# Scores of two heads at once on the halves of TensorE's rows, in float32r parts, with the masks ahead of them

## The chip, the cores and the metric

The kernel runs on one core of a Trainium2 chip, in one launch. The metric is the device time of that core in microseconds (us). Five engines work side by side, each on its own queue of instructions: TensorE (PE in the rows; PEld is its weight load, PEq or PEldq its sequencer), VectorE (DVE), ScalarE (ACT), GpSimd (POOL) and SyncE (SP).

## The reference, cut to what matters

A network of four blocks works on x, 512 tokens of 1024 numbers in float32. The first two blocks (a convolution with a linear recurrence, and differential attention, each followed by a gated feed-forward layer) come first; then two layers follow, each a mixing layer and a layer of experts (MoE) with a layer norm behind each. A mixing layer has sixteen heads of 64 numbers, four of each of four kinds; the three kinds that the change touches are these (the fourth, latent attention or MLA, stays in float32):

```python
def _stick_breaking_attention(q, k, v):            # 4 heads
    z = jnp.einsum('bhqd,bhkd->bhqk', qb, k).astype(jnp.float32) * scale
    before = kpos[None, :] < qpos[:, None]
    log_keep = jnp.where(before, jax.nn.log_sigmoid(-z), 0.0)
    ...
def _forgetting_attention(q, k, v, log_f):         # "Fox", 4 heads
    s = jnp.einsum('bhqd,bhkd->bhqk', qb, k).astype(jnp.float32) * scale
    return s + cb[..., :, None] - c[..., None, :]  # then a causal softmax
    ...
def _dilated_attention(qs, ks, vs):                # 4 heads, 3 branches
    for (window, dil), q, k, v in zip(((128, 1), (512, 4), (2048, 16)), qs, ks, vs):
        idx = qpos[:, None] - dil * jnp.arange(window // dil + 1)[None, :]
        z = jnp.einsum('bqhd,bqnhd->bhqn', qb, kb).astype(jnp.float32) * scale
        p = jnp.exp(jnp.where(valid[None, None], z, -jnp.inf) - m)
    ...
x = _layernorm(DN_ALPHA * x + _mixing(x, ...), ...)
x = _layernorm(DN_ALPHA * x + _hier_moe(x, ...), ...)
```

Queries and keys of the dilated heads are rotated by position (rope) first. Depthwise convolution in the first block has 31 taps.

## The kernel before

Names: P = 128 rows, T = 512 tokens, D = 1024, NT = 4 tiles of tokens, `xs` the four tiles of x (128x1024 each).

**Products in parts.** `split` (L212, L213) writes a float32 tile as two float32r parts: ScalarE copies the high part, VectorE subtracts it to get the low part. `mm3` (L261 to L263) multiplies in three passes, high by high and the two cross terms. Projections, feed-forward and experts run so. The differential attention (L844) has its q and k in parts as well: the two maps of a head lie on rows 0 to 63 and 64 to 127, each pass is issued for the one and then the other, into two PSUM banks, and the masks (L846) follow. `diff_head` is not changed.

**A mixing layer.** `section` projects three times 256 columns: q of four heads, k of four heads, and v. Head h has its q and k on rows 64 (h % 2) and up of column h // 2. `rope2` rotates a projected column with VectorE and GpSimd and writes it into one float32 tile `qk` of `quads`. Scores are then single float32 products over 64 rows: `scores` (L1219, dilated branches 1 and 2, four 128-column tiles in a bank, each with a mask product L1220 behind it), `scores2` (L1238 to L1243, branch 0, two query tiles in a bank), `softmax_heads.scores` (L1524, then the forget row L1526 and the mask L1527; MLA uses it too without the row) and `stick_breaking.scores` (L1563). A mask is a bfloat16 product with the identity. After the scores `exp_rows` takes the maximum on VectorE (L1150) and the exponential on ScalarE (L1155); then TensorE transposes (L1162) and multiplies by v.

**Order.** In the mixing layers TensorE's order is written by hand (`manual_schedule`). `weave` and `fill` lay the small steps of the attention between the projections of the next section, by the costs that `pipelined` is given. The other engines are ordered by the scheduler. PSUM has eight banks; `self.ps("s")` takes the next of a cycle, and before the change "s" and "t" have two banks each. `late_ln` applies the gain of the layer norm before (`gain`, L467, L468) to the four tiles of x on VectorE while the first section runs. At the layer's end `out_add` (L1369) adds the output projection to x.

**Other places.** `conv` block (L608 to L630) does 11 taps of each of four blocks of channels on TensorE, by diagonal matrices that GpSimd (L624) and ScalarE (L625) make, and the rest as VectorE operations (L629). `moe_last` ends a MoE layer: 16 products with a 0/1 matrix `place` (L1838) put the last experts' rows back in order, VectorE adds them to x in halves (L1842), and the layer norm's statistics (L350) follow. Ahead of it stands a branch on how many blocks of tokens there are (L1823). `x<-acc` are DMAs of 512 KB on GpSimd's queue that bring a tile of x from DRAM.

## Time and profile before

| | us |
|---|---|
| median of 3 runs | 2835.93 (2834.44 to 2836.62) |
| the profiled execution | 2840.61 |
| its span | 2838.5 |
| TensorE busy | 2711.8 (96%) |
| VectorE busy | 1661.8 (59%) |
| ScalarE busy | 1292.0 (46%) |
| GpSimd busy | 456.8 (16%) |

In the span, the convolution lies at 20 to 175 us, the two mixing layers at about 1215 to 1650 and 2025 to 2460, and the two MoE layers behind them. A row of the timeline is a run of like instructions of one engine: start, length, line, result and operands, shape, count, and in brackets how long the engine had been idle and what released it. Matmuls overlap and their ends are modelled; the cost of one is the distance from its start to the next start.

### The profile page before, as it was taken

How to read it: one execution, taken by the hardware profiler on the slowest of the kernel's cores; microseconds unless marked ns; L12 is line 12 of the kernel's file. 1: busy time of each engine (PE TensorE's matmuls, PEld its weight loads, DVE VectorE, ACT ScalarE, POOL GpSimd, SP SyncE). 2: the span in 40 equal slices, each digit the busy share in tenths (PEclk: the TensorE clock that was granted, in tenths of full speed). 3: DMA queues.
4: the chain of work that ended last, by engine and by line, in shares of the span. 5: the costliest groups of instructions: out<-in, count | busy, mean ns of one | idle time of the engine just before them, and what ended most of it. 6: DMA issues, size and time to landing. Idle time of an engine off the chain costs nothing. (4 is left out here: it accounts for less than half of the span.)

```text
span 2838.5 us, 40948 instructions
## 1 busy us (share of the span) xinstructions
PE 2711.8 (96%) x14416; PEld 2250.9 (79%) x14416; DVE 1661.8 (59%) x2598; ACT 1292.0 (46%) x2020; POOL 456.8 (16%) x410
## 2 busy tenths in 40 slices
PE   8989999999999999999999969999899999799995
PEld 6768888887678888898877768888787787688885
DVE  7785333377864333464345587578743344756897
ACT  4643222255643222243364336568534544346785
POOL 2314000011113000011020042112101120412113
PEclk9999999999999999999999979999899999899998
DMA  6114323222114223222211058979412111278995
GB/s 222 47 45 163 104 82 104 89 102 79 60 53 141 100 86 104 89 75 75 70 40 60 18 206 278 287 237 332 149 60 86 45 69 33 104 242 258 356 359 197
DMA packets 90248, 376.56 MB, mean 133 GB/s; under 512 B 14352, under 2 KB 15760, under 8 KB 73488
## 3 DMA queue, kind: packets, MB, share of 16 engines
q1 hardware_dynamic: 76304, 329.14, 32.9%
q0 software_dynamic: 11104, 38.93, 5.4%
q10 hardware_dynamic: 2592, 5.49, 0.6%
q8 instruction: 117, 1.92, 0.3%
q14 instruction: 131, 1.07, 0.1%
HBM read 344.96 MB, written 28.57 MB: 132 GB/s over the span
## 5 line engine op out<-in xcount | busy, mean ns | idle before, releaser
L213 DVE TENSOR_TENSOR wpart<-raw,wpart 128x1024 fp32r<-128x1024 f32 (+3 forms) x385 | 519.0, 1378 | 315.9 <-ACT wpart L212 306.8
L212 ACT ACTIVATE wpart<-raw 128x1024 fp32r<-128x1024 f32 (+3 forms) x393 | 446.2, 1170 | 393.8 <-PE mm L262 175.6
L261 PE MATMUL mm<-xT,wpart 128*128 128x512 f32 (+1 forms) x1136 | 443.5, 390 | 12.2 <-ACT wpart L212 8.2
L263 PE MATMUL mm<-xT,wpart 128*128 128x512 f32 (+1 forms) x1136 | 429.3, 378 | 3.1 <-DVE wpart L213 3.1
L262 PE MATMUL mm<-xT,wpart 128*128 128x512 f32 (+1 forms) x1136 | 429.7, 378 | 1.3 <-DVE xT L213 1.3
L261 PEld LDWEIGHTS mm<-xT,wpart 128*128 128x128 f32 x1136 | 216.3, 190 | 51.5 <-ACT wpart L212 8.2
L261 PE MATMUL mm<-wpart,xT 128*128 128x256 f32 (+2 forms) x672 | 256.0, 381 | 0.0
L263 PEld LDWEIGHTS mm<-xT,wpart 128*128 128x128 f32 x1136 | 215.8, 190 | 47.6 <-DVE wpart L213 3.9
L262 PEld LDWEIGHTS mm<-xT,wpart 128*128 128x128 f32 x1136 | 216.5, 191 | 40.9 <-DVE xT L213 2.3
L263 PE MATMUL mm<-wpart,xT 128*128 128x256 f32 (+2 forms) x672 | 241.8, 361 | 0.2 <-DVE xT L213 0.2
L262 PE MATMUL mm<-wpart,xT 128*128 128x256 f32 (+2 forms) x672 | 240.6, 358 | 0.0
L343 POOL TENSOR_TENSOR sm<-sm,mhalf 128x4 f32<-128x4 f32 (+2 forms) x74 | 65.9, 892 | 1069.1 <-DVE sm L354 768.5
L262 PE MATMUL mm<-wpart,gT 128*128 128x256 f32 (+1 forms) x544 | 183.8, 338 | 0.0
L263 PE MATMUL mm<-wpart,gT 128*128 128x256 f32 (+1 forms) x544 | 183.2, 337 | 0.0
L261 PE MATMUL mm<-wpart,gT 128*128 128x256 f32 (+1 forms) x544 | 183.1, 337 | 0.0
L261 PEld LDWEIGHTS mm<-wpart,xT 128*128 128x128 f32 x672 | 145.2, 216 | 19.9 <-issue 7.7
L263 PEld LDWEIGHTS mm<-wpart,xT 128*128 128x128 f32 x672 | 145.0, 216 | 13.8 <-DVE xT L213 1.4
L262 PEld LDWEIGHTS mm<-wpart,xT 128*128 128x128 f32 x672 | 145.5, 217 | 10.1 <-issue 1.2
L544 DVE TENSOR_TENSOR silu<-silu,mm 128x512 f32<-128x512 f32 x44 | 30.2, 687 | 203.0 <-PE mm L263 203.0
L213 DVE TENSOR_TENSOR xT<-raw,xT 128x1024 fp32r<-128x1024 f32 x108 | 130.1, 1221 | 15.2 <-ACT xT L212 14.6
L1150 DVE TENSOR_REDUCE sm<-s 128x1 f32<-128x128 f32 (+3 forms) x96 | 53.3, 555 | 119.7 <-PE s L1220 45.7
L212 ACT ACTIVATE xT<-raw 128x1024 fp32r<-128x1024 f32 x108 | 111.8, 1053 | 8.2 <-DMA raw<-in_w_dram 7.6
(549 smaller groups left out, 5739.4 us busy)
## 6 DMA issues: line engine op xcount, KB each, us to landing
raw<-in_w_dram SPq DMA_DIRECT2D x324, 512.0 KB
raw<-in_gu_dram SPq DMA_DIRECT2D x40, 1024.0 KB
raw<-in_w_in_dram SPq DMA_DIRECT2D x30, 1024.0 KB
raw<-in_down_dram SPq DMA_DIRECT2D x16, 1024.0 KB
raw<-in_o_qk_dram SPq DMA_DIRECT2D x8, 1024.0 KB
raw<-in_w_out_dram SPq DMA_DIRECT2D x8, 1024.0 KB
raw<-in_e_in_dram SPq DMA_DIRECT2D x7, 1024.0 KB
raw<-in_down_dram SPq DMA_DIRECT2D x8, 768.0 KB
```

Of the source, the lines that this page charges most:

```text
L212: ins = self.nc.scalar.activation(hi, x, AF.Copy)
L213: self.last_lo = (eng or self.nc.vector).tensor_sub(lo, x, hi)
L261: mm(out, lhsT=ls[0], rhs=rs[0], start=start, stop=False)
L262: mm(out, lhsT=ls[0], rhs=rs[1], start=False, stop=False)
L263: mm(out, lhsT=ls[1], rhs=rs[0], start=False, stop=stop)
L343: self.last_rsqrt = self.nc.gpsimd.tensor_tensor(v, v, self.half[:, :n], op=ALU.pow)
L544: nc.vector.tensor_mul(s, s, ps[2 * j + 1])
L1150: nc.vector.tensor_reduce(nm, s.rearrange("p (n c) -> p n c", n=n), axis=AX, op=ALU.max, negate=True)
```

## The change

1. `section` keeps q and k as float32r parts in four tiles per buffer and two buffers; `rope2` and the plain sections end in a `split`.
2. `scores3` does the scores of two heads at once: masks first (with `start=True`), then three passes for each place, head by head in turn on rows 0 to 63 and 64 to 127, into two banks. Dilated branches and Fox use it; the odd head's part is kept in `waiting` until its turn. The stick-breaking heads take three passes one head at a time.
3. After the first section "s" and "t" share one cycle of four banks.
4. x goes to DRAM after `gain` (`lend_x`) and its tiles serve as buffers; `return_x` brings it back from GpSimd's queue, tiles 0 and 1 in `mla_heads.forget`, 2 and 3 after the last turned tile.
5. The last block of the convolution does 15 taps on TensorE instead of 11.
6. `moe_last` adds half 0 of x into PSUM by four float32 products with the identity ahead of the place products; statistics and normalisation read that half from PSUM, and VectorE adds half 1 only.
7. Masks are laid out anew and loaded in eight pieces instead of five; the layer norm's rows come as two tiles.

```diff
-NBUF = 15
+NBUF = 11
...
-    add("m_causal", np.where(k <= q, 0, neg))
...
-    add("m_all", np.full((P, P), neg))
+    causal = np.where(k <= q, 0, neg)
+    add("m_first", np.concatenate([np.full((P, P), neg), causal], axis=1))
+    _CF["m_causal"] = (_CF["m_first"][0] + P, P)
+    add("m_band", np.concatenate([np.where(k >= q, 0, neg), causal], axis=1))
...
-            raw = pool.tile([P, nm // 5], F32, name="rawc")
-            for h in range(5):
-                cs = slice(h * nm // 5, (h + 1) * nm // 5)
+            raw = pool.tile([P, nm // 8], F32, name="rawc")
+            for h in range(8):
+                cs = slice(h * nm // 8, (h + 1) * nm // 8)
...
-        for h, x in enumerate(self.x_halves(i)):
+        for h, x in enumerate(self.x_sources(i)):
...
+    def x_sources(self, i):
+        return [self.sums.get((i, h), x) for h, x in enumerate(self.x_halves(i))]
...
+    def norm_halves(self, i, rs, nm):
+        for src, x in zip(self.x_sources(i), self.x_halves(i)):
+            self.nc.scalar.activation(x, src, AF.Identity, bias=nm, scale=rs)
+        self.sums.pop((i, 0))
...
+        taps = PTAPS + (4 if j == 3 else 0)
+        n = T + taps - 1
...
-        for k in range(PTAPS):
+        ws = [pool.tile([P, PTAPS + 4], F32R, tag=f"taps{i}", name=self.uid("taps"))[:, :taps] for i in range(2)]
+        self.split(*ws, self.cols[:, _COLS["conv_w"] + j * 31:_COLS["conv_w"] + j * 31 + taps])
+        for k in range(taps):
...
-            self.mm3(ps, d, [t[:, k:k + T] for t in pads], k == 0, k == PTAPS - 1)
-        nc.vector.tensor_scalar(cv, pad[:, PTAPS:PTAPS + T], w(PTAPS), self.col("conv_b", j), op0=ALU.mult, op1=ALU.add)
-        for k in range(PTAPS + 1, 31):
+            self.mm3(ps, d, [t[:, k:k + T] for t in pads], k == 0, k == taps - 1)
+        nc.vector.tensor_scalar(cv, pad[:, taps:taps + T], w(taps), self.col("conv_b", j), op0=ALU.mult, op1=ALU.add)
+        for k in range(taps + 1, 31):
...
-            self.free, self.quads, self.outs = tiles(NBUF, [T]), tiles(3, [4, T]), tiles(4, [1056])
+            self.free, self.outs = tiles(NBUF, [T]), tiles(4, [1056])
...
                 self.weave(s1.steps)
+                self.bank["s"] = self.bank["t"] = cycle(range(2, 6))
                 gain()
-                s2 = self.section(xT, (3, 4, 5), rope=True, classes=True)
+                self.lend_x()
+                s2 = self.section(xT, (3, 4, 5), 1, rope=True, classes=True)
...
+    def quad_tile(self, n, j, shape, dtype=F32):
+        return self.pool.tile([P] + shape, dtype, tag=f"quad{n}{j}", name=self.uid("qd"))
...
+    def lend_x(self):
+        self.x_kept = self.dram.tile([T, D], F32, name=self.uid("xk"))
+        for i, x in enumerate(self.xs):
+            self.nc.gpsimd.dma_start(self.x_kept[i * P:(i + 1) * P, :], x)
+        self.lent = [x for i in range(2) for x in self.x_halves(i)]
+        self.spare = [x for i in range(2, NT) for x in self.x_halves(i)]
+        self.free += self.spare
+    def return_x(self, tiles):
+        for i in tiles:
+            self.nc.gpsimd.dma_start(self.xs[i], self.x_kept[i * P:(i + 1) * P, :])
...
+            parts = r.qk[j][:, 0], r.qk[j][:, 1]
             if rope:
-                self.rope2(ps[j], r.qk[:, j], classes, 0.125 if j < 2 else 1.0)
+                self.rope2(ps[j], parts, classes, 0.125 if j < 2 else 1.0)
             elif j < 2:
-                nc.scalar.activation(r.qk[:, j], ps[j], AF.Copy, scale=0.125)
+                self.split_scaled(*parts, ps[j], 0.125)
             else:
-                nc.vector.tensor_copy(r.qk[:, j], ps[j])
+                self.split(*parts, ps[j])
...
-        u = (t, sh)
-        if parts:
-            nc.vector.tensor_add(t, *u)
-            self.split(*out, t)
-            self.drop(sh, t)
-            return
+        nc.vector.tensor_add(t, t, sh)
         if classes:
-            out = out.rearrange("p (r j) -> p j r", r=4)
-            u = [x.rearrange("p (j r) -> p j r", r=4) for x in u]
-        nc.vector.tensor_add(out, *u)
+            parts = [x.rearrange("p (r j) -> p j r", r=4) for x in parts]
+            self.split(*parts, t.rearrange("p (j r) -> p j r", r=4))
+        else:
+            self.split(*parts, t)
         self.drop(sh, t)
+    def scores3(self, banks, h, qk, place, mask):
+        mm = self.nc.tensor.matmul
+        q, k = qk[h // 2], qk[2 + h // 2]
+        for m, s in enumerate(banks):
+            mask(h + m, s)
+        for cs, qs, ks in place:
+            for n, (a, b) in enumerate(((0, 0), (0, 1), (1, 0))):
+                for m, s in enumerate(banks):
+                    rows = slice(64 * m, 64 * m + 64)
+                    mm(s[:, cs], lhsT=q[rows, a, qs], rhs=k[rows, b, ks], start=False,
+                       stop=n == 2 and cs == place[-1][0])
...
         def scores(h):
-            q, k = begin(h)
-            s = self.ps("s")
-            for i in range(NT):
-                cs = slice(i * P, (i + 1) * P)
-                mm(s[:, cs], lhsT=q[:, cs], rhs=k[:, cs], start=True, stop=False)
-                mm(s[:, cs], lhsT=self.identb, rhs=self.mask("m_causal" if br == 1 else "m_mod4"), start=False, stop=True)
-            if h == 3:
-                self.quads.append(sec.qk)
-            return self.exp_rows(s, r.ns[:, h], NT), NT
+            if h % 2:
+                return waiting.pop(h)
+            begin()
+            banks = [self.ps("s") for _ in range(2)]
+            mask = self.mask("m_causal" if br == 1 else "m_mod4").unsqueeze(1).to_broadcast([P, NT, P])
+            self.scores3(banks, h, sec.qk, [(tile_cs(i),) * 3 for i in range(NT)],
+                         lambda _, s: mm(s.rearrange("p (i c) -> p i c", i=NT), lhsT=self.identb, rhs=mask, start=True,
+                                         stop=False))
+            p = [(self.exp_rows(s, r.ns[:, h + m], NT), NT) for m, s in enumerate(banks)]
+            waiting[h + 1] = p[1]
+            return p[0]
...
+            def mask(_, s):
+                if i2:
+                    mm(s.rearrange("p (i c) -> p i c", i=2), lhsT=self.identb,
+                       rhs=self.mask("m_band").unsqueeze(1).to_broadcast([P, 2, 256]), start=True, stop=False)
                 else:
-                    mm(s[:, c0:c0 + P], lhsT=self.identb, rhs=self.mask("m_all"), start=True, stop=True)
-                    mm(s[:, c0 + P:c0 + 256], lhsT=qs, rhs=k[:, :P], start=True, stop=False)
-                mm(s[:, c0 + P:c0 + 256], lhsT=self.identb, rhs=self.mask("m_causal"), start=False, stop=True)
-            if (h, i2) == (3, 1):
-                self.quads.append(sec.qk)
-            return self.exp_rows(s, r.ns[:, h, 2 * i2:2 * i2 + 2], 2), 4
+                    mm(s, lhsT=self.identb, rhs=self.mask("m_first", 512), start=True, stop=False)
...
-            r.steps = self.pipelined([(h,) for h in range(4)], lambda h: (1.1, 0.43, 0.4), scores, values)
+            r.steps = self.pipelined([(h,) for h in range(4)], lambda h: (1.1, 0.7, 0.7), scores, values)
         else:
-            r.steps = self.pipelined([(h, i) for h in range(4) for i in range(2)], lambda h, i: (1.1, 0.43, 0.4),
-                                     scores2, values2)
+            r.steps = self.pipelined([(h + m, i) for h in (0, 2) for i in range(2) for m in range(2)],
+                                     lambda h, i: (1.1, 0.7, 0.7), scores2, values2)
...
-            self.drop(*mla.mt)
-            r.qT, r.kT, r.v = self.quads.pop(0), self.quads.pop(0), self.vs.pop(0)
...
-                self.drop(*r.cT, *r.u)
+                self.drop(*r.cT)
+                self.return_x(range(2, NT))
...
+        def scores_row(h, i):
+            if h % 2:
+                return waiting.pop((h, i))
+            n = (i + 1) * P
+            banks = [self.ps("s")[:, :n] for _ in range(2)]
+            def mask(h, s):
+                mm(s, lhsT=self.mask("sel")[:96, h * P:(h + 1) * P], rhs=row.crow[:, :n], start=True, stop=False)
+                causal(s, i)
+            self.scores3(banks, h, sec.qk, [(slice(0, n), slice(i * P, n), slice(0, n))], mask)
+            p = [(self.exp_rows(s, self.sm([P, 1]), 1), i + 1) for s in banks]
+            waiting[h + 1, i] = p[1]
+            return p[0]
...
+            r.units = [(h + m, i, scores_row, values) for h in (0, 2) for i in range(NT) for m in range(2)]
...
-            s = ss[u] = self.ps("st"[u % 2])
-            mm(s[:, :n], lhsT=k[:, j * P:(j + 1) * P], rhs=q[:, j * P:], start=True, stop=True)
+            s = ss[u] = self.ps("s")
+            for m, (a, b) in enumerate(((0, 0), (0, 1), (1, 0))):
+                mm(s[:, :n], lhsT=k[rows, a, j * P:(j + 1) * P], rhs=q[rows, b, j * P:], start=m == 0, stop=m == 2)
...
+        for i in range(NT):
+            self.nc.tensor.matmul(ps[i][0], lhsT=self.ident, rhs=self.xs[i][:, :T], start=True, stop=False)
...
-                    self.nc.tensor.matmul(p, lhsT=self.place[:, i], rhs=t[:, c * T:(c + 1) * T], start=n == 0, stop=n == 1)
+                    self.nc.tensor.matmul(p, lhsT=self.place[:, i], rhs=t[:, c * T:(c + 1) * T],
+                                          start=c == 1 and n == 0, stop=n == 1)
         def add(i, h):
+            if h == 0:
+                self.sums[i, h] = ps[i][h]
+                return
```

On TensorE, at the first two heads of dilated branch 1 in the first mixing layer (mm is a projection, s the bank of scores, mx the tile of q and k, cb the masks), before:

```order
L263 MATMUL mm_8636<-wpart_87,xT_73 128x256
L1219 MATMUL s_8696<-mx_8277 128x128
L1220 LDWEIGHTS identb
L1220 MATMUL s_8696<-cb,identb 128x128
L1219 MATMUL s_8696<-mx_8277 128x128
L1220 LDWEIGHTS identb
```

and after (qd are the tiles of parts):

```order
L265 MATMUL mm_8673<-wpart_87,xT_73 128x256
L1271 LDWEIGHTS identb
L1271 MATMUL s_8739<-cb,identb 128x512
L1271 LDWEIGHTS identb
L1271 MATMUL s_8740<-cb,identb 128x512
L1193 MATMUL s_8739<-qd_8330,qd_8328 128x128
L1193 MATMUL s_8740<-qd_8330,qd_8328 128x128
```

The masks of two heads, 512 columns each, now stand ahead of all scores; the passes of the two heads alternate (24 in all, of which two are shown), and no projection stands between the two heads.

On TensorE in Fox, at a 384-column unit (t is the bank of transposes, o that of the product with v), before:

```order
L1524 MATMUL s_11196<-mx_8278 128x384
L1526 LDWEIGHTS cb
L1526 MATMUL s_11196<-cp_10380,cb 128x384
L1527 LDWEIGHTS identb
L1527 MATMUL s_11196<-cb,identb 128x128
L261 MATMUL mm_11138<-wpart_83,xT_72 128x512
L262 MATMUL mm_11138<-wpart_84,xT_72 128x512
L263 MATMUL mm_11138<-wpart_83,xT_73 128x512
L1162 MATMUL t_11207<-cf,mx_8276 128x128 x2
```

and after, from the last two passes of a pair on:

```order
L1193 MATMUL s_11248<-qd_10425,qd_10423 128x384
L1193 MATMUL s_11249<-qd_10425,qd_10423 128x384
L1211 MATMUL t_11266<-cf,mx_8292 128x128 x2
L1615 MATMUL o_11233<-mx_8308,mx_8302 128x65 x2
L1407 MATMUL t_11272<-cf,mx_8303 128x128 x4
L1407 MATMUL t_11279<-cf,mx_8303 128x128 x4
L1211 MATMUL t_11286<-cf,mx_8300 128x128 x3
```

Both heads' scores are done before anything else; behind them come the transposes of a unit before (L1211, two), its product with v, eight transposes of finished heads (L1407), and then the three transposes of the pair's even head.

On TensorE at the end of the first MoE layer (mm banks, gT the last experts' rows in parts, rt the matrix `place`), before:

```order
L263 MATMUL mm_18808<-xT_72,hT_11676 128x512
L1823 UNCONDITIONAL_BRANCH x16
L1838 MATMUL mm_18988<-gT_11673,rt_11911 128x512
L1838 MATMUL mm_18990<-gT_11673,rt_11911 128x512
L1838 MATMUL mm_18992<-gT_11673,rt_11911 128x512
```

and after (cf holds the identity):

```order
L265 MATMUL mm_19019<-xT_72,hT_11887 128x512
L1904 UNCONDITIONAL_BRANCH x16
L1914 MATMUL mm_19199<-x_74,cf 128x512
L1914 MATMUL mm_19201<-x_75,cf 128x512
L1914 MATMUL mm_19203<-x_76,cf 128x512
L1914 MATMUL mm_19205<-x_77,cf 128x512
L1922 MATMUL mm_19199<-gT_11884,rt_12122 128x512
L1922 MATMUL mm_19199<-gT_11885,rt_12122 128x512
```

The four identity products stand behind the branch and ahead of the first place product, and the place products now end one bank after the other.

## Rows read from the trace of the kernel before

**Rows 1.** Stretches: us, busy (count) PE PEld DVE ACT POOL, clock, DMA, GB/s.

```profile
1210.00:1640.00 430.00, 427.88 (x2423) 353.22 (x2422) 210.92 (x408) 186.81 (x373) 59.14 (x85) 1.00 0.16 56
2020.00:2460.00 440.00, 434.14 (x2452) 359.35 (x2452) 220.80 (x419) 187.09 (x370) 68.67 (x90) 0.98 0.18 62
...
1215.00:1261.00 46.00, 46.00 (x302) 46.00 (x301) 36.06 (x48) 18.14 (x29) 5.88 (x7) 1.00 0.26 92
```

**Rows 2.** Timeline of PE, first head of branch 1: start, us, then the group.

```profile
1261.60 0.48 PE L1219 MATMUL s<-mx 64*128 64x128 f32 x2
...
1263.79 0.48 PE L261 MATMUL mm<-xT,wpart 128*128 128x512 f32 x1
1264.11 0.39 PE L262 MATMUL mm<-xT,wpart 128*128 128x512 f32 x1
1264.34 0.39 PE L263 MATMUL mm<-xT,wpart 128*128 128x512 f32 x1
```

**Rows 3.** Timeline of PE, differential attention: 128 (two cuts), 256 and 512 columns.

```profile
664.80 0.44 PE L844 MATMUL s<-dr,dr 64*128 64x128 f32 x4
...
664.80 0.55 PE L844 MATMUL s<-dr,dr 64*128 64x128 f32 x6
665.29 0.28 PE L846 MATMUL s<-cb,identb 128*128 128x128 bf16 x2
...
690.42 0.62 PE L844 MATMUL s<-dr,dr 64*128 64x256 f32 x6
690.98 0.29 PE L846 MATMUL s<-cb,identb 128*128 128x128 bf16 x2
...
700.03 0.96 PE L844 MATMUL s<-dr,dr 64*128 64x512 f32 x6
700.92 0.28 PE L846 MATMUL s<-cb,identb 128*128 128x128 bf16 x2
```

**Rows 4.** Timeline of PE, branch 0: two units, each with what follows it.

```profile
1402.07 0.70 PE L1238 MATMUL s<-mx 64*128 64x256 f32 x2
...
1403.63 0.48 PE L261 MATMUL mm<-xT,wpart 128*128 128x512 f32 x1
...
1408.90 0.23 PE L1241 MATMUL s<-cb,identb 128*128 128x128 bf16 x1
...
1410.36 0.36 PE L261 MATMUL mm<-wpart,xT 128*128 128x256 f32 x1
```

**Rows 5.** Timeline of PE, a 512-column unit of Fox.

```profile
1574.47 1.12 PE L1524 MATMUL s<-mx 64*128 64x512 f32 x2
1575.53 0.39 PE L1526 MATMUL s<-cp,cb 96*128 96x512 bf16 x1
1575.76 0.22 PE L1527 MATMUL s<-cb,identb 128*128 128x128 bf16 x1
```

**Rows 6.** Timelines of DVE and ACT, behind the same unit.

```profile
1576.47 0.68 DVE L1150 TENSOR_REDUCE sm<-s 128x1 f32<-128x512 f32 x1
...
1577.25 0.69 ACT L1155 ACTIVATE mx<-s,sm 128x512 f32<-128x512 f32 x1 [1.90 <-DVE sm L1150]
```

**Rows 7.** Timelines of DVE and PE at the end of the convolution.

```profile
153.88 7.37 DVE L629 SCALAR_TENSOR_TENSOR cv<-pad,cols,cv 128x512 f32<-128x512 f32 x11
...
161.90 2.07 PE L716 MATMUL s<-cv,nmean 128*128 128x512 f32 x2 [5.28 <-DVE cv L630]
```

**Rows 8.** End of the second MoE layer: branch, and timelines of PE and DVE.

```profile
L1823 PEldq COMPARE_BRANCH  x2: 193/1881/3569, 2803.0 to 2806.8; - x2
...
2808.56 5.31 PE L1838 MATMUL mm<-gT,rt 128*128 128x512 f32 x16 [4.04 <-ACT gT L212]
...
2811.10 1.42 DVE L1842 TENSOR_TENSOR x<-x,mm 128x512 f32<-128x512 f32 x2 [1.26 <-PE mm L1838]
...
2822.92 0.15 DVE L354 TENSOR_SCALAR sm<-sm 128x1 f32<-128x1 f32 x1
```

**Rows 9.** DMA issues from 2785 us on: KB each, median us to landing.

```profile
x<-acc POOLq DMA_DIRECT2D x4, 512.0 KB, 8.2
```

More of the change, by code (lines that the diff above doesn't have):

```diff
@@ L183, in c, with mask @@
         return self.cf[:, o:o + n]
-    def mask(self, name):
-        o, n = _CF[name]
+    def mask(self, name, n=0):
+        o, n = _CF[name][0], n or _CF[name][1]
         o -= _CF["masks"][0]
@@ L336, in ln_rows @@
     def ln_rows(self, li, t):
+        if isinstance(t, list):
+            for n, row in enumerate(t):
+                self.nc.sync.dma_start(row, self.a["rows"][li:li + 1, n].to_broadcast([P, D]))
+            return t
         self.nc.sync.dma_start(t, self.a["rows"][li:li + 1].to_broadcast([P, 2, D]))
@@ L457, in turn @@
         def turn(i):
-            self.ln_turned(NT - 2 + i, self.late_li, [buf[:, i, :T], buf[:, i, T:]], bank)
+            row = buf[i] if isinstance(buf, list) else buf[:, i]
+            self.ln_turned(NT - 2 + i, self.late_li, [row[:, :T], row[:, T:]], bank)
             self.ln_end = self.last_lo
@@ L495, in last_ln @@
                     rs, nm = next(steps[i - 1])
-                    for x in self.x_halves(i - 1):
-                        nc.scalar.activation(x, x, AF.Identity, bias=nm, scale=rs)
+                    self.norm_halves(i - 1, rs, nm)
                 for job in meanwhile[i]:
@@ L1024, in mixing @@
                               + [(w_out[half, kg], 4) for kg in range(2) for half in range(2)])
-            rows = self.quads[-1].rearrange("p (a b) t -> p a (b t)", a=2)
+            rows = [self.quad_tile(1, j, [D]) for j in range(2)]
             with tc.manual_schedule(engines={tc.nc.tensor.engine}):
                 *turns, gain = self.late_ln(rows, "t")
-                s1 = self.section(xT, (0, 1, 2), rope=True, classes=True, first=turns)
+                s1 = self.section(xT, (0, 1, 2), 0, rope=True, classes=True, first=turns)
                 self.weave(s1.steps)
+                self.bank["s"] = self.bank["t"] = cycle(range(2, 6))
                 gain()
-                s2 = self.section(xT, (3, 4, 5), rope=True, classes=True)
+                self.lend_x()
+                s2 = self.section(xT, (3, 4, 5), 1, rope=True, classes=True)
                 d1 = self.dilated(1, s1)
@@ L1034, in mixing @@
                 n1 = self.natural(d1)
-                s0 = self.section(xT, (6, 7, 8), rope=True)
+                s0 = self.section(xT, (6, 7, 8), 0, rope=True)
                 d2 = self.dilated(2, s2)
@@ L1074, in mixing, with section @@
         self.small = small
-    def section(self, xT, ids, rope=False, classes=False, first=None):
+    def quad_tile(self, n, j, shape, dtype=F32):
[10 more added lines that the diff above has]
+            self.nc.gpsimd.dma_start(self.xs[i], self.x_kept[i * P:(i + 1) * P, :])
+    def section(self, xT, ids, buf, rope=False, classes=False, first=None):
         nc = self.nc
@@ L1084, in column @@
             if (j, k) == (0, 0) and toks.start == 0:
-                r.qk = self.quads.pop(0)
+                r.qk = [self.quad_tile(buf, n, [2, T], F32R) for n in range(4)]
             if k == 0 and toks.start == 0:
@@ L1124, in section, with rope2 @@
         return r
-    def rope2(self, ps, out, classes, scale=1.0, parts=False):
+    def rope2(self, ps, parts, classes, scale=1.0):
         nc = self.nc
@@ L1231, in scores2 @@
         def scores2(h, i2):
[L1232 to L1233 removed]
+            if h % 2:
+                return waiting.pop((h, i2))
+            begin()
+            banks = [self.ps("s") for _ in range(2)]
+            place = []
             for i in (2 * i2, 2 * i2 + 1):
                 c0 = (i % 2) * 256
[L1236 to L1246 removed]
+                j = max(i - 1, 0)
+                place.append((slice(c0 + (P if i == 0 else 0), c0 + 256), tile_cs(i), slice(j * P, (i + 1) * P)))
+            def mask(_, s):
+                if i2:
+                    mm(s.rearrange("p (i c) -> p i c", i=2), lhsT=self.identb,
+                       rhs=self.mask("m_band").unsqueeze(1).to_broadcast([P, 2, 256]), start=True, stop=False)
+                else:
+                    mm(s, lhsT=self.identb, rhs=self.mask("m_first", 512), start=True, stop=False)
+            self.scores3(banks, h, sec.qk, place, mask)
+            p = [(self.exp_rows(s, r.ns[:, h + m, 2 * i2:2 * i2 + 2], 2), 4) for m, s in enumerate(banks)]
+            waiting[h + 1, i2] = p[1]
+            return p[0]
         def values2(h, i2, at):
@@ L1425, in normed @@
             if f == 0:
-                r.cT, r.u = ([self.grab() for _ in range(3)] for _ in range(2))
+                left = [b for b in self.free if not any(b is x for x in self.spare)]
+                assert len(left) + len(self.spare) == len(self.free)
+                self.free = left
+                r.cT, r.u = [self.grab() for _ in range(3)], self.spare[:3]
                 for k, u in enumerate(r.u):
@@ L1437, in forget @@
             self.forget_row(l, mla)
-            self.drop(*mla.mt)
-            r.qT, r.kT, r.v = self.quads.pop(0), self.quads.pop(0), self.vs.pop(0)
+            self.return_x(range(2))
+            r.qT, r.kT = ([self.quad_tile(1, 2 * n + j, [2, T]) for j in range(2)] for n in range(2))
+            r.v = self.vs.pop(0)
         def project(i):
@@ L1512, in forget_row, with softmax_heads @@
         self.drop(*bufs)
-    def softmax_heads(self, sec, q, k, row, end):
+    def softmax_heads(self, sec, row):
         nc = self.nc
@@ L1518, in softmax_heads @@
         r = SimpleNamespace()
-        o = {}
+        o, waiting = {}, {}
+        causal = lambda s, i: mm(s[:, i * P:(i + 1) * P], lhsT=self.identb, rhs=self.mask("m_causal"), start=False,
+                                 stop=row is None)
         def scores(h, i):
@@ L1544, in values @@
             self.head_norm(ov[:, :, :64], ov[:, :, 64], r.o4[:, :, h])
-        r.units = [(h, i, scores, values) for h in range(4) for i in range(NT)]
+        if row is None:
+            r.units = [(h, i, scores, values) for h in range(4) for i in range(NT)]
+        else:
+            r.units = [(h + m, i, scores_row, values) for h in (0, 2) for i in range(NT) for m in range(2)]
         return r
```

54 lines of the change are left out of this document (22 added, 32 removed).

## The prediction

> **What bounds the kernel now.** I read the table of busy times by stretch first. In the first mixing layer TensorE is busy 427.88 of 430 us at full clock; VectorE has 210.92 and ScalarE 186.81, and the second mixing layer reads the same [rows 1]. So a mixing layer lasts as long as TensorE's own instructions, and work taken off TensorE there comes off the time, while work put on VectorE or ScalarE is free as long as it comes early enough. The places outside the mixing layers that the change touches are of another kind: at the end of the convolution and at the end of each MoE layer TensorE waits for others [rows 7, 8].
>
> **Scores of the dilated branches 1 and 2.** A price is read from start to start, since the ends of matmuls are modelled. One head now runs from 1261.60 to 1263.79, 2.19 us: four 64-row float32 products, each with a mask behind it. The neighbours pay too: after a 64-row product the next projection needs 0.32 us (1263.79 to 1264.11) where 0.23 is its usual step [rows 2], 0.09 on leaving, and I take as much on entering. That is 2.37 a head, 4.74 a pair. The new form has no row in these branches, but the differential attention of the same kernel already runs it: six 64-row float32r products, three passes for each of two heads on the two halves of the rows, take 0.49 us with 128 columns, 0.56 with 256 and 0.89 with 512 [rows 3]. So two heads advance together. Inside the 128-column group the third pair of products ends 0.11 us behind the second (0.44 and 0.55 us into it), so that is a step once the group runs. Four tiles are twelve steps: I estimate 0.49 + 9 x 0.11 = 1.5, with 1.96 as the other end (four times the group's 0.49). Two masks, now 512 columns wide and in front, cost 0.23 each by the 512-column bfloat16 product of Fox (1575.53 to 1575.76) [rows 5]: 0.45; leaving and entering 0.18. So 2.13 a pair instead of 4.74, 2.6 saved; two pairs in two branches make **10.4 us a layer** (8.5 at the other end).
>
> **Branch 0.** Two query tiles of a head now take 1.56 us (1402.07 to 1403.63) or, for the first two tiles, 1.46 (1408.90 to 1410.36) [rows 4]; with the neighbours' share 3.3 a head for all four tiles, 6.6 a pair. New: two masks 0.45, six steps of mostly 256 columns about 0.95 (the group's 0.56 and three more of 0.13, an estimate between the 0.11 above and the 0.23 of 512 columns; 1.12 as two whole groups), 0.18 for the change of form: about 1.55, twice a pair, 3.1. Two pairs: **7.0 us a layer** (6.2 at the other end).
>
> **Fox.** A 512-column unit takes 1.06 us for the float32 product and 0.23 for the forget row [rows 5], with the short mask 1.3 in all and 1.5 with the neighbours. A pair in the new form takes 0.89 [rows 3] + 2 x 0.26 + 0.18 = 1.6 instead of 3.0. The narrower units scale between the 128- and 512-column groups of [rows 3]; the four units of a pair sum to 4.6 instead of 8.0, two pairs **6.9 us a layer**. Here something new is late. After a score the row maximum takes 0.68 us on VectorE and the exponential 0.69 on ScalarE, from 1576.47 to 1577.94 [rows 6], and only then can TensorE transpose. In the new order of rows TensorE has about 1.1 to 1.4 us of other work between a pair's last pass and the even head's transposes, with the hops some 0.3 to 0.6 too little at each wide pair, and two banks are emptied where it was one. I take 2.5 us a layer back (0 to 6).
>
> **Stick-breaking** runs one head at a time: one float32 product becomes three float32r passes. At 512 columns that is 1.06 [rows 5] against three steps of 0.23 [rows 2]; at 128 columns three steps of 0.11 to 0.16 [rows 3] stand against 0.42, with hardly a gain. I take 1.1 us a layer, between 0 and 2.4. The Trainium skill, page "TensorE: Matmul & The Clock Gate", section "The mechanism", says that a weight load overlaps running matmuls only where the row group differs; three passes of one head all use the same rows, and by the section "LDWEIGHTS" each load of 128 columns would add an estimated 0.107 us, which leaves nothing of the 1.1. The trace does not bear this out for full rows: the 512-column projections, each with its own load and all rows, stand 0.23 apart [rows 2], so no load shows there; no row shows it for one half.
>
> Sum for a layer: 10.4 + 7.0 + 6.9 + 1.1 - 2.5 = 22.9. Two layers: **46 us** (33 to 54).
>
> **What is put beside it.** Splitting q and k into parts and the wider rope add 20 columns of one ScalarE copy and one or two VectorE operations of about 0.65 us: 10 to 12 us of ScalarE and 11 to 15 of VectorE a layer, against 243 and 219 us of room [rows 1]. Least room is at the layer's start, where VectorE has 36.06 of 46 us [rows 1] and the gains of x now stand four in a row ahead of the rope; the first value column may wait up to 1.5 us a layer, and that is in the range only. x goes to DRAM and back on GpSimd's queue. A DMA of this size lands 8.2 us after its issue [rows 9]; the halves x2 and x3 are sent for after the last turned projection, 10 us or more ahead of their first use in the output sum, so I cost it at nothing; if it were late the output sum would wait and its PSUM banks with it. Three more mask pieces at the start are 0.6 us of VectorE beside a TensorE that waits for something else: nothing, up to 1 us.
>
> **Convolution.** VectorE runs without a gap here, 11 tap operations in 7.37 us, and TensorE waits 5.28 us, until 161.90, for the sum [rows 7]. Four taps of the last block move over: 4 x 0.67 = **2.7 us** less for VectorE. TensorE gets 12 products of 0.23 us = 2.8 (or 3.1, if it waits for four diagonals on GpSimd), which fits into the wait. Between 0 and 3.
>
> **End of the MoE layers.** Four of eight additions on VectorE fall away, 0.7 us each by the two at 2811.10 [rows 8]: 2.7 us of a chain that runs from there to the last statistics at 2822.92. But four float32 identity products stand ahead of the place products on TensorE. They can't start while the branch before them is open: its last row on TensorE is at 2806.80, so 2807.0. At 0.86 to 1.06 us each (four bfloat16 passes of 0.23; the 64-row product of [rows 5] as upper end) they end at 2810.4 to 2811.2, and the place products, now from 2808.56 [rows 8], start some 2 us later. The first addition needs four place products rather than nine, so it starts only 0.2 to 1.8 us later than 2811.10. Net 0.9 to 2.5 less, and about the same at the first MoE layer; I take 1.2 each, **2.4** together (-1 to 5).
>
> **Sum.** 46 + 2.7 + 2.4 = 51.1. The profiled execution took 2840.6 us; it would take 2789.5. The median of the runs is 4.7 us below the profiled one, so **2785 us**. All lower ends together give 2800, all upper ends 2774; with the waits of the layer's start and some reserve for clocks, 2770 to 2802 is this case's own range.
>
> **Rivals.** (a) The halves don't overlap where weights change at each step, and the passes run one behind the other. Then a pair costs 24 x 0.11 + 0.63 = 3.3 in branches 1 and 2 (saves 5.8 a layer), about 4.3 in branch 0 (4.7) and 5.9 in Fox (4.2): 15.7 with the stick's 1, less 2.5, 26 us in two layers, 2805 us. [Rows 3] speak against it: the 0.49 us there hold six products whose weights change too. (b) The mixing layer picks up waits of 5 to 10 us at its start or where x is needed again: 2795 to 2805. Against it stand the room in [rows 1] and the 8.2 us of [rows 9]; for it, that GpSimd's queue and VectorE's gains have become links of one chain. (c) **Slower**: the pairs starve for PSUM banks. Each pair needs two free banks at once; scores and transposes share a cycle of four; and a bank is held until its exponential has ended, 2.2 us after the unit's last product started (1575.76 to 1577.94) [rows 5, 6]. There are 16 such pairs in a layer and as many stick units. From 51 / 32 = 1.6 us of wait for each pair on, the change loses; at 2.2 it costs 70 us and gives 2855. Against it: between two pairs lie several projection products, and four banks hold two pairs. The Trainium skill, page "TensorEngine Tiling (Array Packing)", "Gotcha 1: PSUM Pressure", says the same of row tiles: different row tiles cannot use one bank at the same time; the trace of before has two banks for the two heads of [rows 3] and TensorE goes straight on behind them. (d) A milder form of it, 0.8 to 1.6 us of wait a pair: 2811 to 2836, at its upper end no change.
>
> **How the numbers follow.** Forecast as summed 0.78; (a) 0.07; (b) 0.07; (c) 0.05; (d) 0.03, which I count as no change. The range takes in (a)'s price and most of (b): 2768 to 2806. 0.2% is 5.7 us, about what a measurement of this kernel tells from no change. Faster 0.92, the same 0.03, slower 0.05.
>
> **What would show it.** The pair of branch 1 should take about 2.0 us from its first mask to the next projection, a branch-0 pair 1.5, a 512-column Fox pair 1.5, and waits of TensorE in a mixing layer should stay under 6 us in sum. At the end of the MoE layers the identity products should start at the branch's end, not earlier, and the first addition about a microsecond later than now. The prediction is wrong if a pair takes more than 3 us, if TensorE waits for VectorE's maxima or for x by more than 10 us a layer, or if the second layer gains less than the first.

## The result

The changed kernel has a median of 2795.87 us (2788.31 to 2801.5, 4 runs) beside 2835.18 for the kernel before; the ratio is 0.986 with a 95% interval from 0.9833 to 0.9887, some 40 us. Two later sets of five runs gave 2792.05 and 2792.98 beside 2838.82 and 2837.67 (0.9834 and 0.9848). The forecast was 2785 with 2768 to 2806: the direction and the range held, the middle was 7 to 11 us too low. The execution whose trace is read below was the fastest of its set, 2788.31 us with a span of 2786.5.

The page of the changed kernel, busy times by engine: TensorE's went from 2711.8 to 2664.2.

```profile
PE 2664.2 (96%) x14504; PEld 2232.6 (80%) x14508; DVE 1678.5 (60%) x2621; ACT 1315.5 (47%) x2076; POOL 469.4 (17%) x430
```

Timeline of PE in the changed kernel: the first pair of branch 1, a pair of branch 0 and a 512-column pair of Fox, each from its masks (L1271, L1296, L1603 with L1586) to what follows. They answer to [rows 2, 4, 5].

```profile
1258.58 0.61 PE L1271 MATMUL s<-cb,identb 128*128 128x512 bf16 x2
1259.11 1.55 PE L1193 MATMUL s<-qd,qd 64*128 64x128 f32 x24
1260.60 0.50 PE L263 MATMUL mm<-xT,wpart 128*128 128x512 f32 x1
...
1388.54 0.60 PE L1296 MATMUL s<-cb,identb 128*128 128x512 bf16 x2
1389.07 0.98 PE L1193 MATMUL s<-qd,qd 64*128 64x256 f32 x12
1389.98 0.38 PE L263 MATMUL mm<-wpart,xT 128*128 128x256 f32 x1
...
1558.37 0.38 PE L1603 MATMUL s<-cp,cb 96*128 96x512 bf16 x1
...
1559.01 0.97 PE L1193 MATMUL s<-qd,qd 64*128 64x512 f32 x6
1559.92 0.55 PE L1211 MATMUL t<-cf,mx 128*128 128x128 f32 x3
```

The 24 passes of branch 1 take 1.49 us (1.5 was forecast), the whole pair 2.02; the pair of branch 0 takes 1.44 and that of Fox 1.55.

To see where the time went, I matched like instructions of two traces in their order; the number is how much later they start than in a second trace of the kernel before (e9_before, below), so that a negative number is time gained.

```
at (us of before)             changed   again (e1)  again (e12)
200   convolution over          -1.0      -1.2         +0.5
1225  first mixing layer        -0.7      -1.5         +0.9
1640  its end                  -23.8     -24.7        -22.2
1985  first MoE layer, late    -23.7     -24.2        -22.0
2030  second mixing layer      -25.7     -26.4        -24.1
2460  its end                  -47.3     -48.1        -45.9
2815  end of the program       -48.0     -42.0        -44.1
```

The mixing layers give 23.1 and 21.7 us, the same to 0.1 us in all three traces. Everything else moves by a few us from one execution to the next, most of all the second MoE layer. The 23.1 hold a dip of TensorE's clock in the kernel before, told under e9_before; without it the first layer gives 21.7 as well.

### The profile page after: what moved, and what is told of

Read it like the earlier page. It is cut to its first block, busy times and chain, and to the rows that moved or that the text cites. A ratio compares the mean times of both kernels' runs of the same rounds, so it can differ in the third digit from the quotient of the medians.

```text
span 2786.5 us, 41347 instructions
## 1 busy us (share of the span) xinstructions
PE 2664.2 (96%) x14504; PEld 2232.6 (80%) x14508; DVE 1678.5 (60%) x2621; ACT 1315.5 (47%) x2076; POOL 469.4 (17%) x430
## 5 line engine op out<-in xcount | busy, mean ns | idle before, releaser
L215 DVE TENSOR_TENSOR wpart<-raw,wpart 128x1024 fp32r<-128x1024 f32 (+3 forms) x385 | 525.6, 1395 | 315.1 <-ACT wpart L214 298.9
L215 DVE TENSOR_TENSOR xT<-raw,xT 128x1024 fp32r<-128x1024 f32 x108 | 129.8, 1221 | 17.1 <-ACT xT L214 16.7
L263 PE MATMUL mm<-xT,hT 128*128 128x512 f32 x272 | 114.0, 419 | 1.6 <-ACT xT L214 1.6
```

The source lines that it names most:

```text
L215: self.last_lo = (eng or self.nc.vector).tensor_sub(lo, x, hi)
L263: mm(out, lhsT=ls[0], rhs=rs[0], start=start, stop=False)
```

## The experiments

**The changed kernel again (e1_again, e12_again)**, no edit.

> The changed kernel once more, for a second trace and for its spread: its four runs lie between 2788.3 and 2801.5 us, those of the kernel before between 2833.4 and 2836.6. Theory: the gain sits in the mixing layers and is the same in each run (about 23 us a layer, 2.6 at the convolution, 1 at the end of each MoE layer), and what differs from run to run is added in the MoE layers, where the DMA engines are 88% busy; then this trace agrees with the first one to 0.5 us in both mixing layers, whatever its own time. Rival: x on its way through DRAM comes at varying times; then the mixing layers differ by several us.

> The changed kernel itself beside the two above, on the same chip: 2788 to 2800, with its mixing layers within 0.3 us of those of its first two traces.

Measured: 2792.05 (2791.04 to 2794.35) and 2792.98 (2790.93 to 2796.35); the mixing layers as in the table. So the gain is the mixing layers', and the spread is not: most of it is added in the second MoE layer, where TensorE waits for parts of the expert weights (xT) 4.5 us in e1_again and 2.9 in the first trace, and behind the last branch. x's way through DRAM shows no effect: the returns landed 3.4 to 5.5 us after their issue in the three traces, and the first output sum waited for TensorE, not for x.

**The kernel before again (e9_before)**, no edit.

> The kernel before once more, for a second trace of it. In the first one the clock dips once in the first mixing layer (0.91 from 1321 to 1341 us) and TensorE's eight variance products at the end of the convolution run at half clock (5.4 us); its execution took 2840.6 us where the timed ones have a median of 2837.7. Theory: these dips are chance; without them the mixing layers of before are 1.6 us shorter, so that the change brings 21.5 us a layer, not 23.2, and the time is 2834 to 2839. Rival: the dips belong to the kernel before, and they come again at the same places.

Measured: 2837.12 us. The clock dip came again in the first mixing layer, a little earlier, while TensorE was busy without a gap; the changed kernel has none there. Stretches of the second trace of before, then of the changed kernel (the number after the last engine is the granted clock):

```profile
1305.00:1325.00 20.00, 20.00 (x93) 18.32 (x94) 3.05 (x3) 5.61 (x11) 1.41 (x2) 0.91 0.19 60
```

```profile
1305.00:1325.00 20.00, 20.00 (x111) 17.57 (x111) 5.71 (x7) 7.89 (x16) 2.61 (x3) 1.00 0.32 107
```

It costs 1.5 to 1.6 us. Over four traces of unchanged mixing layers (the first trace of before, this one, e5_conv_only and e6_moe_only) it came three times in eight layers: in both layers of the first trace and in the first layer of this one. In the second layer of this trace it is absent, which is why that layer's gain reads 21.7 and not 23.1; against the first layer of e5_conv_only, which has no dip either, the changed kernel's first layer gives 21.7 too. My theory of pure chance is not refuted, nor shown.

**Convolution alone (e5_conv_only), the change without it (e11_conv11).**

```diff
-        taps = PTAPS + (4 if j == 3 else 0)
+        taps = PTAPS                          # e11; e5: the kernel before with the + line of the change
```

> The kernel before with nothing but 15 taps on TensorE in the last block of the convolution. Theory of the prediction: VectorE sets the end there, four operations of 0.67 us less are 2.6 us less from 180 us on, and nothing else moves. Rival, from the traces so far: the run with 11 taps and the changed mixing layers was 2.9 us ahead of the first trace by 180 us as well, so TensorE's place in the order (a product for the variance behind the projections) sets the end, and the taps alone bring 0 to 1 us.

> The changed kernel with 11 taps in all blocks of the convolution. Theory: VectorE's 2.6 us come back, but TensorE then idles longer ahead of 162 us, its clock falls earlier and is back by the variance products, which take 3.7 us instead of 5.4; by 180 us the two kernels stand within 1 us of each other, and so do the times. Rival (the prediction's step): 2.7 us slower.

Measured: 2838.17 beside 2837.70 of before (ratio 1.0003, 0.999 to 1.0015); 2793.84 without the taps beside 2792.98 with them. The taps bring nothing that can be measured. VectorE's part of the step holds: the sum comes earlier and TensorE's wait for it falls from 5.29 to 2.87 us. But behind it stand the four variance products (pmean; each leaves two records, so they read as x8), and TensorE runs them in part at the lower of its two clock levels, 1.2 GHz: the granted clock is 0.64 from 169.6 to 174.4 us in the changed kernel and 1.00 from 171.1 to 174.2 in e11. Timeline of PE, first without the taps (e11), then the changed kernel, answering to [rows 7]:

```profile
160.77 2.08 PE L735 MATMUL s<-cv,nmean 128*128 128x512 f32 x2 [5.29 <-DVE cv L649]
...
171.07 3.70 PE L741 MATMUL s<-gr,pmean 128*128 128x512 f32 x8 [1.84 <-ACT gr L740]
```

```profile
161.41 1.98 PE L735 MATMUL s<-cv,nmean 128*128 128x512 f32 x4 [2.87 <-DVE cv L649]
...
169.59 5.40 PE L741 MATMUL s<-gr,pmean 128*128 128x512 f32 x8 [2.52 <-ACT gr L740]
```

The products start 1.5 us earlier, not 2.7, and take 1.7 longer. In all nine traces with 15 taps they took 5.4 us; of the five with 11 taps three show 3.7 (e11, and e4 and e6 below) and the two of before 5.4 and 5.1: so with 11 taps the clock is back by then in some executions, with 15 in none seen. In four of the nine (e5, e7, e10, e12) the mean's products (nmean) ahead of them take 3.1 to 3.2 us instead of 2.0 as well, and the variance products start at 170.2 to 171.4 us, about where they do with 11 taps.

**MoE ends alone (e6_moe_only), the change without them (e10_moe_add), and another order (e8_inter).** e6 is the kernel before with the identity products, e10 the changed kernel without; e8:

```diff
-        for i in range(NT):
-            self.nc.tensor.matmul(ps[i][0], lhsT=self.ident, ...)
+        ident(0)                      # the same product, for one tile
...
         for i in range(NT):
+            if i + 1 < NT:
+                ident(i + 1)
```

> The kernel before with nothing but the identity products at the end of the MoE layers. Theory: the first addition comes 0.9 us later, VectorE's chain is 2.2 to 2.7 us shorter, so 1 to 1.5 us less at each of the two places, 2 to 3 in sum: 2834 to 2837 where the kernel before has 2838. Rival: the identity products delay the low part of the rows as well and eat the gain: 0.

> The changed kernel, with the additions at the end of the MoE layers back on VectorE and no identity products; the convolution keeps its 15 taps. Theory, from the kernel before with the identity products alone (no change there): within 2 us of the changed kernel of the same call. Rival (the prediction's step): 2.4 us slower.

> The changed kernel with the identity products laid between the place products (two ahead, then one behind each tile) rather than all four ahead. Theory: in the changed kernel the first addition waits for four identity products; with two it comes 1.5 us earlier at the end of each MoE layer, about 2.5 us in sum: 2789 to 2792 where the changed kernel has 2792. Rival: VectorE's split of the low part of the rows is what is late (it started 2.2 us behind ScalarE's high part there, 0.7 in the kernel before), for another reason: no change.

Measured: e6 2839.25 beside 2837.70 (ratio 1.0007, 0.9997 to 1.0018), nothing; e10 2797.37 beside 2792.98 with overlapping runs (2793.06 to 2801.82), and its trace lost 2.3 us in a feed-forward layer that the edit doesn't touch; e8 2789.69 (2788.34 to 2792.77) with a ratio of 0.9838, no better than e1's 0.9834. The step itself is seen in the traces. Changed kernel, end of the second MoE layer, PE and then DVE, answering to [rows 8]; and the same place in e12_again, PE:

```profile
2755.94 3.70 PE L1914 MATMUL mm<-x,cf 128*128 128x512 f32 x8 [2.85 <-ACTq L1904]
2759.07 4.24 PE L1922 MATMUL mm<-gT,rt 128*128 128x512 f32 x16
...
2758.49 1.29 DVE L215 TENSOR_TENSOR gT<-ym,gT 128x512 fp32r<-128x512 f32 x2 [5.77 <-PE mm L1914]
2760.61 0.69 DVE L1930 TENSOR_TENSOR x<-x,mm 128x512 f32<-128x512 f32 x1 [0.82 <-PE mm L1922]
```

```profile
2758.15 5.40 PE L1914 MATMUL mm<-x,cf 128*128 128x512 f32 x8 [3.15 <-ACTq L1904]
2762.98 4.24 PE L1922 MATMUL mm<-gT,rt 128*128 128x512 f32 x16
```

The identity products start at the branch's end, as forecast; the four (eight records) take 3.1 us at full clock (granted 1.00), but 4.8 where the clock falls under them (granted 0.64, in e12_again). VectorE's split of the low part (L215) now stands behind them. From the last expert product to the last statistics it is 18.5 us in both traces of before, and 17.3, 19.4 and 19.3 in three of the changed kernel, 20.8 in e6: nothing gained on average. At the first MoE layer it is 23.4 and 24.0 before, 22.1 to 22.9 with the identity products: 1.4 us gained. The kernels with changed mixing layers and without identity products lose another 3 us there, in which ScalarE waits behind the branch for nothing that the profile shows (timeline of ACT, e10):

```profile
1976.06 1.15 ACT L214 ACTIVATE gT<-ym 128x512 fp32r<-128x512 f32 x2 [4.81 <-issue]
```

What it waits for stays open. In e8 the first addition at the end of the first MoE layer comes 9.1 us behind the last expert product instead of 10.0, but the last statistics come 23.4 us behind it instead of 22.3: VectorE takes up other work (L215, L401) before the last tile.

**The mixing layers alone (e4_mix_only)**, e10's and e11's edits together.

> The changed kernel with the convolution at 11 taps for all blocks and the MoE layers' last additions on VectorE, as before the change; the mixing layers are the changed ones. Theory: the parts add up, so its trace is 2.6 us slower by the end of the convolution, 0.9 and 1.2 at the two MoE layers, 4.7 in sum: 2793 for an execution like the first profiled one (2788.3), 2800 in the median. Its spread should be as wide as that of the changed kernel if the mixing layers bring it, and 3 us if the identity products do.

Measured: 2795.54 (2794.40 to 2797.24) beside 2792.05 of e1_again: 3.5 slower, near the 4.7, but for another reason than the sum: its trace is level with e1's after the convolution (-1.3 and -1.2 by 200 us) and loses 3.5 us from 1985 to 2030 us, where e1_again gains 2.2, by the wait at ScalarE just shown (6.13 us there).

**Passes in blocks (e2_serial).**

```diff
+        for m, s in enumerate(banks):
             for cs, qs, ks in place:
                 for n, (a, b) in enumerate(((0, 0), (0, 1), (1, 0))):
-                for m, s in enumerate(banks):
```

> In a pair the three passes of all places are issued for the first head and then for the second, instead of head by head in turn. Theory: the two halves of the rows run side by side only because neighbours in the queue use different halves; then the 24 products of a branch-1 pair take about 2.7 to 3.0 us instead of 1.49, a 512-column Fox pair 1.6 to 1.8 instead of 0.91, and the time rises by about 13 us a layer, 27 in all: 2815 to 2825. Rival: the halves are not what makes it fast (the float32r passes alone do it): no change, 2790 to 2800.

Measured: 2807.43 (2802.61 to 2810.23), 15 slower than e1 of the same call, but only 5.2 and 4.5 us of that lie in the mixing layers, where I expected 13 each; the rest is lost in places that the edit doesn't touch. Timeline of PE: a branch-1 pair, then a 512-column Fox pair (two windows on the same run of products).

```profile
1261.16 2.50 PE L1193 MATMUL s<-qd,qd 64*128 64x128 f32 x24
1263.59 0.50 PE L263 MATMUL mm<-xT,wpart 128*128 128x512 f32 x1
...
1566.23 0.74 PE L1193 MATMUL s<-qd,qd 64*128 64x512 f32 x4
...
1566.23 0.97 PE L1193 MATMUL s<-qd,qd 64*128 64x512 f32 x6
1567.13 0.33 PE L1211 MATMUL t<-cf,mx 128*128 128x128 f32 x1
```

With twelve products of one head ahead of twelve of the other the pair takes 2.43 us instead of 1.49. With three ahead of three it takes 0.90, like the 0.91 of the alternating order: the second half of the rows starts although products for the first half stand before it in the queue. The shorter of the two windows, which ends at 1566.6 us, already holds four products, more than the three of one head.

**One head at a time (e7_singles).**

```diff
-                    rows = slice(64 * m, 64 * m + 64)
+                    rows = slice(64 * ((h + m) % 2), 64 * ((h + m) % 2) + 64)
...
-            banks = [self.ps("s") for _ in range(2)]     # in scores, scores2 and scores_row
+            banks = [self.ps("s")]
```

> The changed kernel with the scores of one head at a time: float32r parts and masks ahead as in the change, but no pairs. It tells the parts from the pairs. Theory: a head of branch 1 takes 0.23 for its mask, 12 passes at 0.11 and some 0.4 around them, 1.9 us instead of 2.37 before and 1.0 in a pair; half heads of branch 0 about 1.3 instead of 1.65; a 512-column Fox unit about 1.3 instead of 1.5. The parts alone keep 8 to 10 of the 23 us a layer, the pairs bring the other 13 to 15: 2815 to 2825. Rival (the parts do it, pairs add nothing): 2790 to 2797.

Measured: 2821.50 (2818.08 to 2821.76), a ratio of 0.9942 (0.9925 to 0.9959). The mixing layers give 7.8 and 6.3 us against e9_before, instead of 23.1 and 21.7. So the parts with the masks ahead bring 14 us in two layers (12.6 without the dip in e9_before) and the pairs 31. Timeline of PE, one head of branch 1 and one 512-column head of Fox:

```profile
1260.73 0.39 PE L1269 MATMUL s<-cb,identb 128*128 128x512 bf16 x1
1261.05 1.55 PE L1193 MATMUL s<-qd,qd 64*128 64x128 f32 x12
1262.53 0.50 PE L263 MATMUL mm<-xT,wpart 128*128 128x512 f32 x1
...
1573.06 0.96 PE L1193 MATMUL s<-qd,qd 64*128 64x512 f32 x3
1573.96 0.55 PE L1211 MATMUL t<-cf,mx 128*128 128x128 f32 x3
```

Twelve passes of one head take 1.48 us, 24 of two heads 1.49: but for its mask, the second head is free.

**Two banks for the scores again (e3_banks).**

```diff
-                self.bank["s"] = self.bank["t"] = cycle(range(2, 6))
...
-            s = ss[u] = self.ps("s")
+            s = ss[u] = self.ps("st"[u % 2])
```

> The scores have two banks of their own again and the transposes two, instead of one cycle of four for both (the stick-breaking heads alternate between them as before). Theory of starving banks: a pair needs both score banks, so it can start only when the exponentials of the pair before have ended; in Fox, with little other work between two pairs, TensorE would wait 1 to 2 us at each of 8 pairs, and some in branch 0: 10 to 15 us a layer, 2810 to 2825. Rival: there is enough other work between two pairs anyway: within 4 us of the changed kernel.

Measured: 2799.36 (2795.65 to 2801.90). The mixing layers give 20.1 and 18.7 us, 3 less each. Little of it is paid by the pairs. In both layers 2.2 to 2.3 us are lost ahead of Fox, among the heads of latent attention, where the transposes of finished heads (L1406) wait 1.91 us for VectorE, which still reads earlier ones out of one of their two banks; the other 0.6 to 0.7 fall in Fox, where one score (L1602) waits 0.2 for the exponential that empties its bank and one group of transposes (L1210) 1.1 for VectorE, 0.4 in the changed kernel. Timeline of PE in e3, then one row of PE's waits in its first mixing layer (us in total, times, longest):

```profile
1514.53 1.77 PE L1406 MATMUL t<-cf,mx 128*128 128x128 f32 x8 [1.91 <-DVE xT L930]
...
PE s L1602 <- ACT mx L1203: 0.2, 1, 0.2
```

The kernel before, which also has two banks for each, has the same wait (e9_before, first mixing layer, waits of PE):

```profile
PE t L1349 <- DVE xT L911: 1.9, 1, 1.9
```

So the shared cycle of four banks brings some 2 us a layer by itself, at the transposes. Pairs starving for banks, the prediction's slow rival, cost at most 0.7 us a layer even with two banks, where they were given 35: enough projections lie between two pairs.

## Why the prediction was right where it was, and where it was not

- **Scores** (45.8 forecast, 44.8 against e9_before, 46.4 against the first trace): right in mechanism, and in size to about 2 us. The clock dips of the kernel before, one in this base and two in the first trace, stand in no term: against layers without a dip it is 21.7 twice, 43.4, and the closeness of the other two figures is luck. The dip also answers a sign that the prediction had named, that it would be wrong if the second layer gained less than the first: it did, 21.7 beside 23.1, by the dip alone. In the first layer branches 1 and 2 with branch 0 give 18.4 to 18.7 us up to 1423 us, 17 without the dip (17.4 forecast). Fox gives less: the widest pairs save 1.4 each as worked out, but Fox as a whole, from 1540 on, only 3.3 us (6.9 less 2.5 forecast). The giving-back is thus 3.6 rather than 2.5; these waits of PE in the changed kernel's first mixing layer (us in total, times, longest) show 2.0 of it, those of L1615 and L1211 and one of L1407, and the rest is not found:

```profile
PE s L427 <- DVE x L1427: 1.9, 1, 1.9
PE o L1615 <- DVE mx L1398: 1.4, 2, 1.2
PE mm L263 <- DVE qd L930: 1.3, 1, 1.3
PE t L1211 <- ACT mx L1204: 0.4, 1, 0.4
PE t L1407 <- ACT mx L1204: 0.4, 2, 0.2
```

  The transposes wait 0.4 us, as thought; the longest wait in Fox is for a scaling on VectorE (L1398) that is late behind the denser units. The first row, for the layer norm at the end, stands in the kernel before as well. The third is new and lies ahead of Fox: a projection waits for VectorE's low part of a column of q or k (qd), where the prediction put the splits at nothing. It costs 1.5 us a layer, and the transposes of finished heads, which no longer wait 1.9 us, give as much back. Both terms were missing from the sum, and that they cancel is luck too.
- **Stick-breaking** (1.1 forecast): about 1.2 from 1423 to 1477 us. Three passes of one half with 512 columns take 0.90 us in e7 where the float32 product took 1.06 [rows 5]. The Trainium skill, page "TensorE: Matmul & The Clock Gate", section "The mechanism", in its sentence on which loads overlap running products (only those of another row group), would let none overlap there. The trace does not agree: the third pass starts 0.23 us behind the second, the step of full rows in [rows 2], and its load lies inside the second (e7, 512-column head of Fox, narrow windows on PE and PEld):

```profile
1573.40 0.39 PE L1193 MATMUL s<-qd,qd 64*128 64x512 f32 x1
1573.63 0.40 PE L1193 MATMUL s<-qd,qd 64*128 64x512 f32 x1
...
1573.40 0.18 PEld L1193 LDWEIGHTS s<-qd,qd 64*128 64x128 f32 x1
```

- **Rival (a), no overlap**: refuted by e7 and the 1.49. **Rival (b), x late or the layer's start**: x's return has slack, and no wait stands at the start; nothing of it is seen. **Rivals (c) and (d), banks**: e3 puts the price at 0.7 us a layer or less, with two banks for the scores.
- **Convolution** (2.7 forecast): failed. The step "TensorE's products fit into the wait" was right by its durations and wrong by its clock: of the 2.7 us 1.5 or less reach the variance products, and these run in part at 1.2 GHz and give 1.7 us back. e5 shows 0.
- **MoE ends** (2.4 forecast): 1.4 at the first, nothing at the second. The sum took 0.86 to 1.06 us for an identity product (its own four passes of 0.23 would make 0.92); they took 0.78 or, with the clock down, 1.2. It also left out that VectorE's split of the low part now waits for them (2758.49 above, 2.2 us behind ScalarE's high part, 0.7 before).
- **The sum**: 43.4 to 46.4, as the clock dips fall, + 0 + 1.4 instead of 51.1, and the forecast's 2785 becomes 2788 to 2791. What is left to 2792 to 2796 lies in the spread between executions, most of it in the last MoE layer, and in the kernel before, whose later medians are 2837.7 to 2838.8 where the prediction set out from 2835.9; it can't be given to a step. The lower ends that the prediction names add up to 2804, not 2800; the range doesn't rest on it.

## What to carry to other kernels

Scores over 64 rows leave half of TensorE unused: with a second head on the other half, issued close behind, it costs nothing more, as long as two PSUM banks are free for each pair. Where TensorE is busy without gaps, such a gain can be summed from start-to-start distances and arrived here to 1.2 us in 22.9 a layer, helped by two waits of 1 to 2 us that nobody had summed and that cancelled. Where TensorE waits, it can't: work moved into a wait can change the clock of what comes behind, as it did here, so there a term of a few us should be given a range down to nothing, and be tried alone. And a gain measured against one trace of the kernel before holds that trace's clock dips: a second trace tells them apart.

## What had not been expected of the hardware

- The halves of the rows take their products independently, and not strictly in the order of the queue: with three products for the first half ahead of three for the other, both halves were done in 0.90 us, as with alternation; with twelve ahead of twelve the overlap is partial (2.43 us against 1.49 and 2.96).
- TensorE's clock fell in the middle of stretches in which it was busy without a gap (granted 0.91 over 20 us), only in kernels with single 64-row float32 products, three times in eight such layers, and in none of the six paired layers of the table above. In e3_banks it falls inside the mixing layers too, but right behind a wait of 1.91 us. The cause stays open.
- In executions of the same kernel the identity products at the end of the second MoE layer ran at the full clock behind a wait of 2.85 us (granted 1.00, 0.78 us each) and in part at half of it behind one of 3.15 us (granted 0.64, 1.2 us each).
